# The last operand sums of a short-convolution kernel's head, chained through PSUM banks

## The chip, the cores and the metric

The kernel runs on one core of a Trainium2 chip. The metric is the device time of one execution in microseconds; less is better. Engines are named as in the profile: PE (TensorE), DVE (VectorE), ACT (ScalarE), POOL (GpSimd), SP (SyncE, which here only issues DMAs). Each engine works through its own queue in order; across engines an instruction waits on semaphores.

## What is computed

One layer, a gated short convolution between two RMS norms, in float32, for 1024 positions of width 1024:

```python
u = rms_norm(x, pre_norm)
z, bg, cg, v = jnp.split(u @ w_in, 4, axis=-1)       # w_in: 1024 x 8192
y = bg * causal_dwconv(cg * v, conv_w) * silu(z)     # 3 taps, 2048 channels
out = x + rms_norm(y @ w_out, post_norm)             # w_out: 2048 x 1024
```

## The kernel before

**Splitting.** A float32 product is made of three matmuls (`pass3`, lines 122 to 125): each operand is split into a high part (`high_u`, a cast on ACT) and a low part (`low_u`, a subtraction on DVE or POOL), and low x high, high x low and high x high add up in a PSUM bank.

**Head.** x is normalised, transposed on PE and kept as eight blocks bgh of [128, 2, 512] (g: a quarter of the 1024 inputs, h: a half of the positions); `read_k` makes a block's high part on ACT and its low part on DVE out of the transposes' PSUM banks pk, and `rebuild_a` copies the sum of both back from the bank into xa or xb (h = 0 or 1) on ACT; for h = 0 `rebuild` does it from the two parts on POOL. Meanwhile the first four column groups of w_in (the four kinds of the first 128 channels) are multiplied in full (`plain`, banks pp). All this is written out by hand as one program order, lines 591 to 719.

**Triples.** The other 60 column groups are taken in 20 triples. A triple's product, 2 halves by 4 quarters by 3 groups, is made of 20 products in place of 24, each of a sum of weight blocks (wA to wJ, two products each, split by `split_w`) and a sum of blocks of x, the form u_i. Seven of the 20 take a block as it is (`UNIT`, `B`); 13 need a form: 7, 9, 5 and 8, made in PSUM from the transposes' banks (`form`, `turned`), and 0, 17, 6, 4, 11, 16, 10, 2 and 19, kept as raw sums in SBUF. `stage(i)` names the place of such a sum: two to a tile by the table `PLACE`, in the pool `up`, which has 18 buffers and also holds the blocks, the forms' split parts u_i and the first weights; 19 stands in a buffer of the pool `raw`. `make` (lines 572 to 575) computes a sum, half by half. The forms of `LATE` (6, 4, 11, 16, 10, 2, 19) are split during the first triple, one after every second product (lines 811 to 815), so their raw sums live until then, and each later u_i takes the buffer of `up` that comes free. In PSUM there are eight banks, handed on in turn.

**The seam.** At line 720 the head's pool is closed; the weights' tiles wA and on take the room of xa and xb. So wA's cast on ACT (line 223) waits for the last sum that reads xa or xb. Then come the weights of the first triple (A to D), the gate and the three convolution taps of the first 128 channels (lines 728 to 735) and the first triple's products in the order `ORDER_0`: 7, 9, 1, 8, 3, 5, 14, 18, 0, 13, 17, 6, 4, 11, 15, 16, 10, 2, 12, 19, each adding into one of the banks pX, pY, pV, pZ, pW (`CHAINS`). `read` takes a bank's interim state off (lines 334 to 355), and the next product into that bank waits for the read. Two of these reads come up below: g <- pX ahead of product 18, and gc <- pY ahead of product 15.

Of the kernel before, what the change touches and what calls it, by code (L numbers as in the profile page):

```python
# [12 lines left out]
ALU = mybir.AluOpType  # L13
# [6 lines left out]
def kernel(  # L20
# [11 lines left out]
    nc = tc.nc  # L32
    P = 128
    _, L, D = x.shape
# [28 lines left out]
    def bank(name):  # L63
        return psum.tile([P, HB], F32, tag="bank", name=name)
# [44 lines left out]
    def new_u(name):  # L109
        return up.tile([P, 2, 2, HB], F32R, tag="u", name=name)  # L110
# [48 lines left out]
    def sums(t, steps):  # L159

        if t >= len(TRIPLES):
            return
        w0, w1, w2 = (ws[t, j] for j in range(3))
        if t not in es:
            es[t] = EP[t % 2].tile([P, 6, FC], F32, tag="e", name=f"e_{t}")
        e = es[t]
        add, sub = nc.gpsimd.tensor_add, nc.gpsimd.tensor_sub
        todo = {
            0: lambda: (add(w2[:, 0], w2[:, 0], w2[:, 1]), add(w2[:, 2], w2[:, 1], w2[:, 2])),  # L169
            1: lambda: sub(e[:, 0:2], w2[:, 0::2], w0[:, 0::2]),  # L170
            2: lambda: sub(e[:, 2], e[:, 1], w0[:, 3]),
            3: lambda: add(w1[:, 2], w2[:, 2], w1[:, 2]),
            4: lambda: sub(e[:, 3], w1[:, 2], w1[:, 0]),
            5: lambda: (sub(w0[:, 2], e[:, 3], w0[:, 2]), sub(w0[:, 0], e[:, 3], w0[:, 0])),  # L174
            6: lambda: sub(w0[:, 2], w0[:, 2], w0[:, 3]),
            7: lambda: sub(e[:, 4], w2[:, 1], w2[:, 3]),
            8: lambda: sub(e[:, 5], e[:, 4], w1[:, 3]),
            9: lambda: add(w2[:, 3], w1[:, 3], w2[:, 3]),
            10: lambda: sub(w1[:, 3], w1[:, 3], e[:, 2]),
            11: lambda: sub(w2[:, 3], e[:, 0], w2[:, 3]),  # L180
            12: lambda: sub(e[:, 3], e[:, 5], w1[:, 0]),  # L181
            13: lambda: add(w1[:, 0], w1[:, 0], w1[:, 1]),
            14: lambda: sub(e[:, 2], e[:, 0], w0[:, 3]),
            15: lambda: sub(w0[:, 3], w0[:, 3], w0[:, 1]),
        }
        for s in steps:
            todo[s]()
# [55 lines left out]
    def wide(pool, tag, name):  # L243
        return pool.tile([P, TAPS - 1 + HB], F32, tag=tag, name=name, bufs=5)

    def inner(t):
        return t[:, TAPS - 1 :]
# [31 lines left out]
    def cv_of(c, h):  # L279
        return inner(gts[c, h])  # L280
# [13 lines left out]
    def pad(c):  # L294
        nc.gpsimd.tensor_copy(gts[c, 1][:, : TAPS - 1], gts[c, 0][:, HB:])

    def gate_g(c, h, src, sign, direct):
        g = cv_of(c, h)
        if direct:
            nc.vector.scalar_tensor_tensor(g, src, float(sign), g, op0=ALU.mult, op1=ALU.mult)  # L300
        else:
            nc.gpsimd.tensor_mul(g, src, g)  # L302
        if h == 0:
            pad(c)
# [122 lines left out]
    gcol = small.tile([P, NK], F32, tag="gcol", name="gcol", bufs=1)  # L427
# [9 lines left out]
    gneg = snp.tile([P, 24], F32, tag="gneg", name="gneg", bufs=1)  # L437
# [35 lines left out]
    def read_k(k, h):  # L473

        g, kk = k // 2, k % 2
        if kk == 0:
            B[g, h] = new_u(f"b{g}{h}")
        u, src, gc = B[g, h], pk[k, h], gcol[:, k : k + 1]
        nc.scalar.activation(u[:, 0, kk], src, AF.Copy, scale=gc)
        nc.vector.scalar_tensor_tensor(u[:, 1, kk], src, gc, u[:, 0, kk].bitcast(F32), op0=ALU.mult, op1=ALU.subtract)  # L480

    def by_tile(a):
        return a.rearrange("p (t l) -> p t l", t=TH)
# [7 lines left out]
    def block(g, h):  # L491
        return (xa, xb)[h][:, :, 2 * g * P : 2 * (g + 1) * P].rearrange("p t (k l) -> p k t l", k=2)

    def as_block(u):
        return u.rearrange("p k (t l) -> p k t l", t=TH)

    plain_w, plain_ps, plain_k = {}, {}, {}
# [13 lines left out]
    def plain(n, h, ks):  # L511

        w = plain_w[n]
        for k in ks:
            first = (n, h) not in plain_ps
            if first:
                plain_ps[n, h] = bank(f"pp_{n}_{h}")
                plain_k[n, h] = 0
            plain_k[n, h] += 1
            hi, lo = (w[:, z, k * P : (k + 1) * P] for z in (0, 1))  # L520
            pass3(plain_ps[n, h], hi, lo, B[k // 2, h], k % 2, first, plain_k[n, h] == NK)

    def snap(n, h, gate=False):
        t = wide(snp, "sn", f"sp_{n}_{h}")
        if gate:
            gts[0, h] = t
        nc.scalar.activation(inner(t), plain_ps[n, h], AF.Silu if n == 2 else AF.Copy)
        return inner(t)
# [4 lines left out]
                turn(k, t)  # L533

    STAGE = {}
    PLACE = {0: (0, 0), 17: (0, 1), 6: (1, 0), 4: (1, 1), 11: (2, 0), 16: (2, 1), 10: (3, 0), 2: (3, 1)}

    def stage(i):
        if i == 19:
            if i not in STAGE:  # L540
                STAGE[i] = raw.tile([P, 2, HB], F32, tag="raw", name="s_19")
            return as_block(STAGE[i])
        n, j = PLACE[i]
        if n not in STAGE:
            STAGE[n] = up.tile([P, 2, 2, HB], F32, tag="u", name=f"s_{n}")
        return as_block(STAGE[n][:, j])

    FORM = {}

    def form(i, make, at=None):  # L550
        FORM[i] = at or [bank(f"f_{i}_{kk}") for kk in range(2)]
        for kk in range(2):
            make(by_tile(FORM[i][kk]), kk)

    def high_u(i):
        U[i] = u = new_u(f"u_{i}")
        for kk in range(2):
            if i in FORM:
                nc.scalar.copy(u[:, 0, kk], FORM[i][kk])
            else:  # L560
                nc.scalar.copy(as_block(u[:, 0])[:, kk], stage(i)[:, kk])

    def low_u(i, eng=nc.vector):
        u = U[i]
        for kk in range(2):
            if i in FORM:
                nc.vector.tensor_sub(u[:, 1, kk], FORM[i][kk], u[:, 0, kk].bitcast(F32))
            else:
                eng.tensor_sub(as_block(u[:, 1])[:, kk], stage(i)[:, kk], as_block(u[:, 0])[:, kk].bitcast(F32))
        FORM.pop(i, None)  # L570

    def make(eng, dst, kind, a, b):

        for kk in range(2):
            (eng.tensor_add if kind == "+" else eng.tensor_sub)(dst[:, kk], a[:, kk], b[:, kk])

    def turned(k, n, other, op):

        def do(dst, kk):
            nc.vector.scalar_tensor_tensor(dst, by_tile(pk[k + kk, 1]), n[:, k + kk : k + kk + 1], other[:, kk], op0=ALU.mult, op1=op)  # L580

        return do
# [4 lines left out]
    b00, b10, b20, b30 = (block(g, 0) for g in range(4))  # L587
    b01, b11, b21, b31 = (block(g, 1) for g in range(4))
# [83 lines left out]
    turn2((0, 1))  # L672
    for k in (0, 1):
        read_k(k, 1)
    low_u(5)
    plain(3, 0, range(KH, NK))
    turn2((6, 7))
# [1 line left out]
        rebuild_a(k, 1)  # L679
    for k in (6, 7):  # L680
        read_k(k, 1)
    form(8, lambda dst, kk: nc.vector.tensor_add(dst, b00[:, kk], b20[:, kk]))
    sn0[3] = snap(3, 0)
    plain(0, 1, (4, 5, 0, 1))
# [12 lines left out]
    for k in (2, 3):  # L697
        rebuild(nc.gpsimd, k, 0)
    make(nc.gpsimd, stage(0), "-", b30, b20)
    make(nc.gpsimd, b10, "+", b10, stage(0))  # L700
    form("q", turned(2, gcol, b21, ALU.subtract))
    q = [by_tile(a) for a in FORM.pop("q")]
    for n in (2, 3):
        plain(n, 1, (4, 5, 0, 1, 6, 7, 2, 3))
    for kk in range(2):
        nc.vector.tensor_add(stage(19)[:, kk], q[kk], b31[:, kk])
    for kk in range(2):
        nc.vector.tensor_sub(stage(16)[:, kk], q[kk], b01[:, kk])
    make(nc.vector, stage(6), "-", b01, stage(19))
    make(nc.vector, stage(17), "+", stage(6), b30)  # L710
    make(nc.vector, stage(11), "-", stage(6), b00)
    make(nc.gpsimd, stage(4), "-", b31, b30)
    make(nc.vector, stage(2), "+", stage(11), b10)
    make(nc.vector, stage(10), "-", b00, b01)
    nc.gpsimd.tensor_mul(inner(gts[0, 0]), inner(gts[0, 0]), sn0[1])
    snap(0, 1, True)
    pad(0)
    high_u(0)
    low_u(0, nc.gpsimd)
# [5 lines left out]
        split_w(0, unit)  # L725
        run_lows()
    sums(0, range(12, 16))
    gate_g(0, 1, plain_ps[1, 1], 1, True)
    high_u(17)
    low_u(17, nc.gpsimd)  # L730
    first_tap(0, 0)
# [256 lines left out]
```

## Time and profile before

| | us |
|---|---|
| median of 3 runs | 783.01 (782.99 to 783.21) |
| the profiled execution | 782.63 |
| its span in the trace | 780.8 |
| PE busy / DVE / ACT / POOL | 762.8 / 494.5 / 447.7 / 465.7 |
| mean granted clock of PE | 0.997 |

A row of a timeline has the start from the span's beginning, the length in us, engine, line, operation, output <- inputs and count; a row with x2 covers two instructions from the first start to the last end. In brackets stands the engine's idle time before it and what ended it. Names are without buffer numbers: s is a raw sum, f a form in PSUM, u a split form, b a block. A row of the groups has the busy time, the mean ns of one and the idle time before them.

### The profile page before, as it was taken

The numbers are of one execution on the slowest core, as the hardware profiler recorded it, in microseconds if no ns is written. First come the engines' busy times: TensorE is split into PE (matmuls) and PEld (weight loads), VectorE is DVE, ScalarE is ACT, GpSimd is POOL, SyncE is SP. The second block draws the span as 40 slices with busy tenths as digits, with TensorE's granted clock in tenths as the row PEclk, the third lists the DMA queues.
The fourth block names the chain that finished last, engine by engine and source line by source line (L and its number), as shares of the span: only waits on it lengthen the run. The fifth ranks groups of instructions, "written<-read, shape, count | busy, mean of one in ns | idle before, by whom it ended". The sixth has DMA issues, their size and how long they took to land.

```text
span 780.8 us, 10022 instructions
## 1 busy us (share of the span) xinstructions
PE 762.8 (98%) x3394; PEld 628.7 (81%) x3394; DVE 494.5 (63%) x750; ACT 447.7 (57%) x873; POOL 465.7 (60%) x565
## 2 busy tenths in 40 slices
PE   8998799999999999999999999999999999999996
PEld 8886588888888888888888888888888888888885
DVE  6898965656567566556565655565664957544756
ACT  7746665566565566645665755566565636544531
POOL 0698677687679669577877987896783320000020
PEclk9999999999999999999999999999999999999999
DMA  9400235536636445356368366665445779754237
GB/s 333 127 0 28 89 86 163 121 99 149 157 95 162 135 108 167 82 160 152 89 122 214 61 177 140 147 158 114 121 101 136 237 234 380 281 185 179 99 121 258
DMA packets 103219, 116.55 MB, mean 149 GB/s; under 512 B 4680, under 2 KB 70272, under 8 KB 102144
## 3 DMA queue, kind: packets, MB, share of 16 engines
q1 hardware_dynamic: 93936, 99.13, 38.6%
q0 software_dynamic: 9216, 16.78, 13.8%
q8 instruction: 26, 0.43, 0.2%
q14 instruction: 25, 0.20, 0.1%
q10 hardware_dynamic: 16, 0.00, 0.0%
HBM read 97.02 MB, written 44.04 MB: 181 GB/s over the span
## 4 chain that ended last, share of the span: by engine, by line
PE 89%; DVE 5%; ACT 4%; issue 1%; DMA 0%; DVEq 0%; ACTq 0%
PE pX L124 8%; PE pX L125 8%; PE pX L123 8%; PE pY L123 7%; PE pY L124 7%; PE pY L125 7%; PE po_x L865 4%; PE po_x L866 4%; PE po_x L867 4%; PE pV L123 3%; PE pV L124 3%; PE pV L125 3%; PE pZ L124 2%; PE pZ L123 2%; PE pZ L125 2%; PE pW L124 2%
## 5 line engine op out<-in xcount | busy, mean ns | idle before, releaser
L905 POOL TENSOR_TENSOR res<-xr,res 128x512 f32<-128x512 f32 x4 | 6.9, 1720 | 105.6 <-DVE res L904 105.6
L329 POOL TENSOR_TENSOR g<-g,sn 128x512 f32<-128x512 f32 x29 | 40.1, 1390 | 45.5 <-ACT sn L327 35.3
L353 DVE TENSOR_TENSOR sn<-sn,pY 128x512 f32<-128x512 f32 x57 | 39.2, 687 | 36.0 <-PE pY L125 21.7
L353 DVE TENSOR_TENSOR sn<-sn,pX 128x512 f32<-128x512 f32 x57 | 39.2, 688 | 34.9 <-PE pX L125 34.9
L302 POOL TENSOR_TENSOR g<-sn,g 128x512 f32<-128x512 f32 x23 | 29.9, 1301 | 47.5 <-DVE sn L351 47.5
L327 ACT ACTIVATE sn<-sn 128x512 f32<-128x512 f32 x24 | 15.2, 632 | 64.1 <-DVE sn L353 40.1
L311 POOL TENSOR_TENSOR g<-g,sn 128x512 f32<-128x512 f32 x20 | 28.2, 1412 | 18.0 <-DVE sn L353 17.7
L345 ACT COPY sn<-pZ 128x512 f32<-128x512 f32 x19 | 11.2, 589 | 46.6 <-PE pZ L125 44.0
L347 ACT ACTIVATE sn<-pV 128x512 f32<-128x512 f32 x38 | 20.7, 599 | 28.7 <-PE pV L125 28.7
L169 POOL TENSOR_TENSOR raw<-raw 128x256 f32<-128x256 f32 x40 | 32.6, 933 | 0.0
L359 POOL DMA_DIRECT2D s_d<-s_d x24 | 19.8, 825 | 21.0 <-DMA s_d<-y_d 13.4
L174 POOL TENSOR_TENSOR raw<-e,raw 128x256 f32<-128x256 f32 x40 | 29.2, 752 | 1.6
L351 DVE TENSOR_TENSOR g<-pY,g 128x512 f32<-128x512 f32 x15 | 10.4, 692 | 30.7 <-PE pY L125 30.7
L170 POOL TENSOR_TENSOR e<-raw,raw 128x512 f32<-128x512 f32 x20 | 25.9, 1294 | 1.6
L123 PE MATMUL pp<-b,wn 128*128 128x512 f32 x64 | 25.8, 403 | 0.1
L874 ACT ACTIVATE jk<-res 128x512 bf16<-128x512 f32 x12 | 7.6, 631 | 31.7 <-DVE res L932 13.0
L124 PE MATMUL pp<-b,wn 128*128 128x512 f32 x64 | 25.1, 393 | 0.4 <-DVE b L480 0.3
L125 PE MATMUL pp<-b,wn 128*128 128x512 f32 x64 | 25.0, 391 | 0.0
L181 POOL TENSOR_TENSOR e<-e,raw 128x256 f32<-128x256 f32 x20 | 14.8, 740 | 16.1 <-ACT wB L219 16.1
L292 DVE SCALAR_TENSOR_TENSOR g<-g,cw,cv 128x512 f32<-128x512 f32 x30 | 22.5, 749 | 1.8
L224 DVE TENSOR_TENSOR wD<-wD,wD 128x512 fp32r<-128x512 f32 x20 | 13.7, 684 | 15.0 <-ACT wD L223 15.0
L292 DVE SCALAR_TENSOR_TENSOR cv<-g,cw,cv 128x512 f32<-128x512 f32 x30 | 22.4, 748 | 0.0
(371 smaller groups left out, 2915.7 us busy)
## 6 DMA issues: line engine op xcount, KB each, us to landing
raw<-in_sc_w_in SPq DMA_DIRECT2D x64, 512.0 KB, 4.4
t_d<-in_sc_w_out SPq DMA_DIRECT2D x32, 256.0 KB, 4.6
s_d<-g SPq DMA_DIRECT2D x29, 256.0 KB, 2.1
s_d<-s_d POOLq DMA_DIRECT2D x24, 256.0 KB, 4.4
y_d<-g SPq DMA_DIRECT2D x23, 256.0 KB, 2.5
t_d<-in_sc_w_out POOLq DMA_DIRECT2D x16, 256.0 KB, 7.7
t_d<-t_d POOLq DMA_DIRECT2D x16, 256.0 KB, 4.5
xr<-in_x SPq DMA_DIRECT2D x8, 512.0 KB, 4.8
```

The lines of the kernel that those rows point to most:

```text
L123: nc.tensor.matmul(ps, lo, u[:, 0, kk], start=first, stop=False, skip_group_check=True)
L124: nc.tensor.matmul(ps, hi, u[:, 1, kk], start=False, stop=False, skip_group_check=True)
L125: nc.tensor.matmul(ps, hi, u[:, 0, kk], start=False, stop=last, skip_group_check=True)
L169: 0: lambda: (add(w2[:, 0], w2[:, 0], w2[:, 1]), add(w2[:, 2], w2[:, 1], w2[:, 2])),
L174: 5: lambda: (sub(w0[:, 2], e[:, 3], w0[:, 2]), sub(w0[:, 0], e[:, 3], w0[:, 0])),
L292: nc.vector.scalar_tensor_tensor(g if j == TAPS - 1 else ps, g, tap(c, j), ps, op0=ALU.mult, op1=ALU.add)
L302: nc.gpsimd.tensor_mul(g, src, g)
L329: when([(c, "cv", h), (c, "silu", h)], (c, "z", h), {"cv": 1, "silu": 1}, lambda: nc.gpsimd.tensor_mul(cv_of(c, h), cv_of(c, h), t))
L353: nc.vector.tensor_sub(a, a, ps)
L865: nc.tensor.matmul(ps, lo, u[:, 0, k % 2], start=first, stop=False, skip_group_check=True)
L866: nc.tensor.matmul(ps, hi, u[:, 1, k % 2], start=False, stop=False, skip_group_check=True)
L867: nc.tensor.matmul(ps, hi, u[:, 0, k % 2], start=False, stop=last, skip_group_check=True)
```

## The change

Forms 10 and 4 (b00 - b01 and b31 - b30) are made early, straight from the transposes' banks, behind `read_k` of the same block: two `scalar_tensor_tensor` each on DVE, the bank times the norm's weight (or its negative) plus or minus the other block. The sums 19, 6 and 11, each of which the next one uses, are made in PSUM banks (`banks_of`), the next sum reads the bank, and ACT copies the bank to the sum's place in SBUF (`keep`). The sum 4 is gone from POOL and the sum 10 from the end on DVE. The gate product of the first 128 channels' second half (`gate_g` at line 728) becomes a plain product on DVE between sums 17 and 11, and `snap(0, 1)` on ACT, which it needs, moves ahead of the sums. `PLACE` pairs the sums anew.

```diff
-    PLACE = {0: (0, 0), 17: (0, 1), 6: (1, 0), 4: (1, 1), 11: (2, 0), 16: (2, 1), 10: (3, 0), 2: (3, 1)}
+    PLACE = {10: (0, 0), 4: (0, 1), 0: (1, 0), 16: (1, 1), 6: (2, 0), 17: (2, 1), 11: (3, 0), 2: (3, 1)}
...
         for kk in range(2):
-            (eng.tensor_add if kind == "+" else eng.tensor_sub)(dst[:, kk], a[:, kk], b[:, kk])
+            d, x, y = (z[kk] if isinstance(z, list) else z[:, kk] for z in (dst, a, b))
+            (eng.tensor_add if kind == "+" else eng.tensor_sub)(d, x, y)
+
+    def keep(i):
+        for kk in range(2):
+            nc.scalar.copy(stage(i)[:, kk], by_tile(FORM[i][kk]))
+
+    def in_bank(i):
+        return [by_tile(a) for a in FORM[i]]
...
     for k in (0, 1):
         read_k(k, 1)
+    for kk in range(2):
+        turned(0, gneg, b00, ALU.add)(stage(10)[:, kk], kk)
     low_u(5)
...
     for k in (6, 7):
         read_k(k, 1)
+    for kk in range(2):
+        turned(6, gcol, b30, ALU.subtract)(stage(4)[:, kk], kk)
...
-    q = [by_tile(a) for a in FORM.pop("q")]
+    q = in_bank("q")
     for n in (2, 3):
         plain(n, 1, (4, 5, 0, 1, 6, 7, 2, 3))
-    for kk in range(2):
-        nc.vector.tensor_add(stage(19)[:, kk], q[kk], b31[:, kk])
-    for kk in range(2):
-        nc.vector.tensor_sub(stage(16)[:, kk], q[kk], b01[:, kk])
-    make(nc.vector, stage(6), "-", b01, stage(19))
-    make(nc.vector, stage(17), "+", stage(6), b30)
-    make(nc.vector, stage(11), "-", stage(6), b00)
-    make(nc.gpsimd, stage(4), "-", b31, b30)
-    make(nc.vector, stage(2), "+", stage(11), b10)
-    make(nc.vector, stage(10), "-", b00, b01)
+
+    def banks_of(i):
+        FORM[i] = [bank(f"f_{i}_{kk}") for kk in range(2)]
+        return in_bank(i)
+
+    snap(0, 1, True)
+    f19 = banks_of(19)
+    make(nc.vector, f19, "+", q, b31)
+    make(nc.vector, stage(16), "-", q, b01)
+    keep(19)
+    f6 = banks_of(6)
+    make(nc.vector, f6, "-", b01, f19)
+    keep(6)
+    make(nc.vector, stage(17), "+", f6, b30)
+    nc.vector.tensor_mul(cv_of(0, 1), plain_ps[1, 1], cv_of(0, 1))
+    f11 = banks_of(11)
+    make(nc.vector, f11, "-", f6, b00)
+    keep(11)
+    make(nc.vector, stage(2), "+", f11, b10)
+    FORM.clear()
     nc.gpsimd.tensor_mul(inner(gts[0, 0]), inner(gts[0, 0]), sn0[1])
-    snap(0, 1, True)
...
-    gate_g(0, 1, plain_ps[1, 1], 1, True)
```

**DVE, behind the reads of blocks b01 and b31 in the head.** Before (b_455 and b_486 are these blocks' low parts, u_429 is u_5, f_0_491 and f_1_492 are form 8):

```order
L480 SCALAR_TENSOR_TENSOR b_455<-pk_1_450,gcol,b_455 128x512
L567 TENSOR_TENSOR u_429<-pk_1_354,u_429 128x512
L567 TENSOR_TENSOR u_429<-pk_1_359,u_429 128x512
L480 SCALAR_TENSOR_TENSOR b_486<-pk_1_474,gcol,b_486 128x512
L480 SCALAR_TENSOR_TENSOR b_486<-pk_1_479,gcol,b_486 128x512
L682 TENSOR_TENSOR f_0_491<-xa 128x512
```

And now (s_460 is the tile of forms 10 and 4):

```order
L480 SCALAR_TENSOR_TENSOR b_455<-pk_1_450,gcol,b_455 128x512
L588 SCALAR_TENSOR_TENSOR s_460<-pk_1_445,gneg,xa 128x512
L588 SCALAR_TENSOR_TENSOR s_460<-pk_1_450,gneg,xa 128x512
L567 TENSOR_TENSOR u_429<-pk_1_354,u_429 128x512
L567 TENSOR_TENSOR u_429<-pk_1_359,u_429 128x512
L480 SCALAR_TENSOR_TENSOR b_489<-pk_1_477,gcol,b_489 128x512
L480 SCALAR_TENSOR_TENSOR b_489<-pk_1_482,gcol,b_489 128x512
L588 SCALAR_TENSOR_TENSOR s_460<-pk_1_477,gcol,xa 128x512
L588 SCALAR_TENSOR_TENSOR s_460<-pk_1_482,gcol,xa 128x512
L694 TENSOR_TENSOR f_0_496<-xa 128x512
```

Two operations stand ahead of u_5's low part, which frees two banks for PE, and two more ahead of form 8.

**DVE, the end of the head.** Before (s_651 is the tile of 6 and 4, s_586 that of 0 and 17, s_648 of 11 and 16, s_660 of 10 and 2):

```order
L575 TENSOR_TENSOR s_651<-xb,s_645 128x512 x2
L575 TENSOR_TENSOR s_586<-s_651,xa 128x512 x2
L575 TENSOR_TENSOR s_648<-s_651,xa 128x512 x2
L575 TENSOR_TENSOR s_660<-s_648,xa 128x512 x2
L575 TENSOR_TENSOR s_660<-xa,xb 128x512 x2
L224 TENSOR_TENSOR wA_684<-wA_685,wA_684 128x512
```

And now (f_0_661 and f_1_662 are sum 6 in its banks, f_0_671 and f_1_672 sum 11):

```order
L576 TENSOR_TENSOR f_0_661<-xb,f_0_652 128x512
L576 TENSOR_TENSOR f_1_662<-xb,f_1_653 128x512
L576 TENSOR_TENSOR s_665<-f_0_661,xa 128x512
L576 TENSOR_TENSOR s_665<-f_1_662,xa 128x512
L731 TENSOR_TENSOR sp_1_650<-pp_1_543,sp_1_650 128x512
L576 TENSOR_TENSOR f_0_671<-f_0_661,xa 128x512
L576 TENSOR_TENSOR f_1_672<-f_1_662,xa 128x512
L576 TENSOR_TENSOR s_675<-f_0_671,xa 128x512
L576 TENSOR_TENSOR s_675<-f_1_672,xa 128x512
L224 TENSOR_TENSOR wA_697<-wA_698,wA_697 128x512
```

Every sum has one input in a bank, the last pair is gone, and the gate product stands among them.

**ACT, between the last reads of the head and wA's cast.** Now (s_658, s_665 and s_675 are the places of 19, 6 and 11; u_682 is u_0); the six copies of L580 are new, and before the change u_0's casts and wA's copies stood right behind `snap(0, 1)`, the first row:

```order
L527 ACTIVATE sp_1_650<-pp_1_502 128x512
L580 COPY s_658<-f_0_652 128x512
L580 COPY s_658<-f_1_653 128x512
L580 COPY s_665<-f_0_661 128x512
L580 COPY s_665<-f_1_662 128x512
L580 COPY s_675<-f_0_671 128x512
L580 COPY s_675<-f_1_672 128x512
L561 CAST u_682<-s_591 128x512 x2
L221 COPY wA_698<-raw_3_140 128x256
L222 COPY wA_698<-raw_0_142 128x256
L223 CAST wA_697<-wA_698 128x512
```

So u_0's casts and wA's copies now come behind all the waits of the copies. Further on, in the first triple, ACT's order is the same, but two casts wait for other buffers: u_10's for DVE's subtraction of u_16, and u_2's, which waited for nothing, for DVE's subtraction of u_10, the last reader of the tile of 10 and 4.

## The prediction

> **What bounds the kernel now.** I read the page first, then the waits of TensorE (PE), then the timeline of each engine where those waits fall.
>
> ```profile
> PE 762.8 (98%) x3394; PEld 628.7 (81%) x3394; DVE 494.5 (63%) x750; ACT 447.7 (57%) x873; POOL 465.7 (60%) x565
> PE pX L123 <- DVE g L351: 3.4, 1, 3.4
> PE pV L123 <- DVE wB L224: 3.1, 1, 3.1
> PE pY L123 <- DVE wE L224: 0.7, 1, 0.7
> PE pY L123 <- DVE gc L353: 0.6, 1, 0.6
> 200.00:400.00 200.00, 199.78 (x881) 164.77 (x880) 119.85 (x182) 117.70 (x248) 148.06 (x187) 1.00 0.51 129
> ```
>
> PE is busy 98% of the span, and between 200 and 400 us (last row: busy PE first) 199.78 of 200. So a change to a helper engine can only win what PE waits, and its long waits are all for VectorE (DVE), all in the seam between the head and the first triple:
>
> ```profile
> 40.65 0.47 PE L123 MATMUL pp<-b,wn 128*128 128x512 f32 x1
> 47.59 0.50 PE L124 MATMUL pp<-b,wn 128*128 128x512 f32 x1
> 63.61 0.39 PE L125 MATMUL pp<-b,wn 128*128 128x512 f32 x1
> 67.09 0.47 PE L123 MATMUL pV<-u,wA 128*128 128x512 f32 x1 [3.10 <-DVE wB L224]
> 81.70 0.50 PE L123 MATMUL pX<-b,wD 128*128 128x512 f32 x1 [3.36 <-DVE g L351]
> 92.10 0.50 PE L123 MATMUL pY<-u,wF 128*128 128x512 f32 x1 [0.64 <-DVE gc L353]
> 94.97 0.39 PE L123 MATMUL pY<-b,wF 128*128 128x512 f32 x1
> ```
>
> Nearly 8 us are waited here. After 92.10 PE never waits again for long, so **the time moves by what the matmul at 92.10 and its next neighbours move**. Before it, DVE has no gap from 75.32 on; before that ScalarE (ACT) has none from 64.60 on, and ACT starts there because the head's last sum on DVE is over:
>
> ```profile
> 39.13 1.28 DVE L567 TENSOR_TENSOR u<-pk,u 128x512 fp32r<-128x512 f32 x2
> 41.22 1.41 DVE L480 SCALAR_TENSOR_TENSOR b<-pk,gcol,b 128x512 fp32r<-128x512 f32 x2 [0.81 <-ACT b L479]
> 42.55 1.83 DVE L682 TENSOR_TENSOR f<-xa 128x512 f32<-128x512 f32 x2
> 46.78 1.41 DVE L480 SCALAR_TENSOR_TENSOR b<-pk,gcol,b 128x512 fp32r<-128x512 f32 x2 [1.06 <-ACT b L479]
> 48.11 1.41 DVE L580 SCALAR_TENSOR_TENSOR f_q<-pk,gcol,xb 128x512 f32<-128x512 f32 x2
> 49.43 1.28 DVE L706 TENSOR_TENSOR s<-f_q,xb 128x512 f32<-128x512 f32 x2
> 50.62 1.28 DVE L708 TENSOR_TENSOR s<-f_q,xb 128x512 f32<-128x512 f32 x2
> 54.12 9.17 DVE L575 TENSOR_TENSOR s<-s,xa 128x512 f32<-128x512 f32 x6
> 63.21 1.28 DVE L575 TENSOR_TENSOR s<-xa,xb 128x512 f32<-128x512 f32 x2
> 53.21 1.14 ACT L561 CAST u<-s 128x512 fp32r<-128x512 f32 x2 [3.55 <-PE pp L125]
> 54.25 0.37 ACT L221 COPY wA<-raw 128x256 f32<-128x256 f32 x1
> 64.60 0.59 ACT L223 CAST wA<-wA 128x512 fp32r<-128x512 f32 x1 [9.57 <-DVE s L575]
> 48.11 2.55 POOL L575 TENSOR_TENSOR s<-xa 128x512 f32<-128x512 f32 x2
> ```
>
> The six sums at 54.12 have both inputs in SBUF and run beside GpSimd (POOL): 9.17 / 6 = 1.53 us each. The two at 63.21, alone, follow each other at about 0.60. L706 and L708 have one input in PSUM and run at (50.62 - 49.43) / 2 = 0.60 each, with POOL's 48.11 row beside them. That difference is what the change can win.
>
> **Step 1, what the two early forms cost.** The four new operations (10 and 4, made from the banks of the transposes) are like L580: (49.43 - 48.11) / 2 = 0.66 each. They stand in the head's tightest part, where DVE, ACT and PE pass banks to each other. The first pair stands before the row of 39.13: that goes to 40.45, its first half is done at 41.15, and PE's matmul of 40.65 needs the bank that it releases: PE +0.5. ACT's two copies out of the same banks now wait for the new pair, its casts behind them move by 0.6, and with them DVE's row of 41.22, to 41.8. Then comes the second pair, so L682 goes from 42.55 to 44.45 (+1.9). It has SBUF inputs and now meets POOL's 512-wide sums in place of 256-wide ones; it took 1.75 for two, its bounds are 1.2 (alone) and 3.06 (as at 54.12), and I take 2.1, near its own row. All behind it is then 2.3 late: ACT's casts of block 1, DVE's row of 46.78 (to 49.1), f_q (to 50.4), and PE, which waits for that row at 47.59 (to 49.9). PE's head ends at 66.15 in place of 63.85. Bounds of this step: 1.4 to 3.3.
>
> **Step 2, the chain.** From 50.4: f_q 2 x 0.66, sums 19 and 16 4 x 0.60, sum 6 2 x 0.60, so sum 6's first half is ready at 54.8. Sum 17 must wait until ACT has copied the half out of its bank (L345, a copy of PSUM to SBUF of the same size, below, has 0.57): it runs at 55.5 and 56.1, ending at 56.8. The gate product (0.60), sum 11 (2 x 0.60), ACT's copy and sum 2 follow; ACT's last copy ends at 59.25, DVE at 60.0, where it ended at 64.5. The two sums at 63.21 (form 10) are gone from DVE, form 4's from POOL. But ACT, a strict queue, now has the six copies ahead of u_0's casts and wA's copies, which it used to do while it waited: 54.25 - 53.21 = 1.04 and 0.8 more (two copies of 0.37, each with its issue), so wA's cast starts at 61.05 in place of 64.60: **3.55 earlier**. ACT, not DVE, sets that.
>
> The price of a sum with an operand or the result in PSUM is from these groups:
>
> ```profile
> L575 DVE TENSOR_TENSOR s<-s,xa 128x512 f32<-128x512 f32 x6 | 9.2, 1592 | 0.0
> L580 DVE SCALAR_TENSOR_TENSOR pk<-pk,gneg,xa 128x512 f32<-128x512 f32 x2 | 1.4, 751 | 0.0
> L575 DVE TENSOR_TENSOR s<-xa,xb 128x512 f32<-128x512 f32 x2 | 1.3, 679 | 0.0
> L708 DVE TENSOR_TENSOR s<-f_q,xb 128x512 f32<-128x512 f32 x2 | 1.3, 680 | 0.0
> ```
>
> PSUM in costs 680 ns against 679, and PSUM in and out 751 for the dearer kind, as its SBUF-bound kin. [...]
>
> **Step 3, the first triple.** ACT from 64.60 and DVE from 75.32 do the same work in the same order, only 3.55 earlier; DVE's gate of a half (0.60) has moved ahead, into the chain, where I counted it. POOL's late work is released by the same casts (wB, u_17) and moves along, so who runs beside whom stays. PE goes from the head straight on at 66.15 (its first product now waits for wA alone), is through product 14 at 75.75 and waits for g until 78.15: 2.4 in place of 3.36. Until then PE, late from step 1, has the least room: ACT's read of pV at 67.7 finds product 7 done with nothing to spare. From 78.15 PE follows DVE, 3.55 early.
>
> **Step 4, a new wait.** The forms have changed buffers: u_2's casts on ACT now take a buffer that DVE's u_10 subtraction must first give up.
>
> ```profile
> 88.87 1.97 DVE L569 TENSOR_TENSOR u<-s,u 128x512 fp32r<-128x512 f32 x2
> 91.97 0.68 DVE L224 TENSOR_TENSOR wI<-wI,wI 128x512 fp32r<-128x512 f32 x1
> 92.57 1.28 DVE L569 TENSOR_TENSOR u<-s,u 128x512 fp32r<-128x512 f32 x2
> 93.86 0.69 DVE L353 TENSOR_TENSOR gc<-gc,pY 128x512 f32<-128x512 f32 x1
> 89.52 1.12 ACT L561 CAST u<-s 128x512 fp32r<-128x512 f32 x2
> 91.59 0.57 ACT L345 COPY gc<-pZ 128x512 f32<-128x512 f32 x1
> ```
>
> In the old clock times: the casts go from 89.52 to 90.9 (end of 88.87's row), behind them wI's two copies end at 93.05 in place of 91.68, so DVE's row of 91.97 goes to 93.1, u_2's pair to 93.7 and the read of pY from 93.86 to 95.0, ending at 95.7. PE's matmul of 94.97 overwrites that bank: it starts at 95.75, with its slow first step **0.9 late**. Bounds: 0 (if something covers it) and 1.4 (the whole delay of the casts). Behind it, by the same reckoning, the next read that PE waits for comes out level with PE, and I find no second stall.
>
> **Sum.** -3.55 + 0.9 = -2.65. The profiled execution took 782.63 (span 780.8): it would be 780.0. The median shown, 783.01, is 0.4 above, so I give 780.4. With step 1 at its bounds the gain is 3.55 or 1.65; with step 4 at 0 it is 3.55.
>
> **Rivals.**
> - *The new wait costs nothing* (something hides it): 3.55 won, 779.5. Against: no slack in the rows above but 0.4 at 94.97. 0.13.
> - *PE becomes the bound.* If the granted clock drops behind the new gaps at 41 and 48 or later, PE arrives late in step 3, where ACT has no room:
>
> ```profile
> 67.40 0.39 PE L124 MATMUL pV<-u,wA 128*128 128x512 f32 x1
> 82.89 0.63 PE L124 MATMUL pX<-b,wD 128*128 128x512 f32 x1
> 80.00:90.00 10.00, 7.59 (x25) 5.75 (x26) 10.00 (x14) 4.34 (x10) 9.84 (x10) 0.83 0.21 79
> ```
>
>   After 3.1 us of waiting the matmuls kept 0.39, after 3.36 they took 0.63 and the slice's clock was 0.83; (1 - 0.83) x 10 = 1.7 us lost. The same loss ahead of product 7 leaves about 1 us of gain: 782.0. My longest gap is 2.4, so it needs a gap longer than I see. [...] 0.12.
> - *The port turns round* (the slower side). From 75.32 on DVE has twelve subtractions with two SBUF inputs, slowed more or less by what POOL does beside them:
>
> ```profile
> L569 DVE TENSOR_TENSOR u<-s,u 128x512 fp32r<-128x512 f32 x12 | 12.8, 1114 | 0.0
> ```
>
>   If POOL does not move along with DVE, they may come out at the 1592 ns of L575: 12 x 0.48 = 5.7 us more on a queue without a gap, so 786; from a mean of about 1335 ns on the gain is gone. (At the 679 of a sum alone they would give 5.2 more.) For it: nothing holds the two engines together but ACT. Against: POOL's work there is released by ACT's casts, as DVE's is. 0.08 beyond 784.6, and 0.07 for a smaller loss that ends within 0.2%.
> - *The chain was not what held ACT*, so nothing is won and the early forms' 2.3 us sit in PE's old slack of 3.1: 783. The wait of 9.57 at 64.60 speaks against it. 0.02.
>
> The forecast has the rest, 0.58. A measurement of this kernel tells about 0.2% (1.6 us) from no change: faster holds the forecast, the first rival and a little of the second (0.73), slower the port (0.08), the same the rest (0.19). The range, 779.0 to 782.5, takes the bounds of steps 1 and 4 and the second rival.
>
> **What would show it.** PE's first product at about 66, not 67.1, with no wait before it; a new wait of 2 us in all at 41 to 50; the chain's sums at 0.68 each, none at 1.5; ACT's wA cast at 61; the wait for g near 2.4, no slice with a lower clock; a new wait of 0.8 before pY<-b,wF near 91.5. I am wrong if L682 takes over 3 us, if the copies leave ACT later than 61.5, or if DVE's subtractions in the first triple change their durations.

## The result and the profile after

The changed kernel takes 780.56 us in the median of seven runs (780.39 to 780.83), against 782.99 (782.44 to 783.42) for the kernel before on the same chip: a ratio of 0.9969, 95% interval 0.9958 to 0.9981. On another chip it was 780.51 against 782.74 (0.9971, 0.9959 to 0.9982). The profiled execution took 780.58 (span 778.8), 2.05 less than that of before. PE's work is the same (first the page's busy times), and so is the middle of the program (then a window, busy PE first, the granted clock, DMA share and GB/s last):

```profile
PE 763.1 (98%) x3394; PEld 629.3 (81%) x3394; DVE 490.6 (63%) x752; ACT 451.2 (58%) x879; POOL 460.0 (59%) x563
```

```profile
200.00:400.00 200.00, 199.78 (x880) 164.81 (x879) 119.77 (x182) 117.78 (x247) 147.57 (x188) 1.00 0.51 130
```

PE's longest waits (us in all, times, the longest):

```profile
PE pX L123 <- DVE g L351: 2.3, 1, 2.3
PE pp L123 <- ACT b L479: 1.8, 2, 1.7
PE pY L123 <- DVE gc L353: 1.2, 2, 0.7
```

The 3.1 ahead of the first product is gone, the one for g is shorter, and there is a new one of 1.8 in the head. The timeline of PE has them in order:

```profile
49.68 0.49 PE L123 MATMUL pp<-b,wn 128*128 128x512 f32 x1 [1.66 <-ACT b L479]
50.47 0.50 PE L124 MATMUL pp<-b,wn 128*128 128x512 f32 x1 [0.29 <-DVE b L480]
...
66.68 0.39 PE L123 MATMUL pV<-u,wA 128*128 128x512 f32 x1
...
78.66 0.50 PE L123 MATMUL pX<-b,wD 128*128 128x512 f32 x1 [2.30 <-DVE g L351]
...
89.06 0.50 PE L123 MATMUL pY<-u,wF 128*128 128x512 f32 x1 [0.67 <-DVE gc L353]
...
92.60 0.50 PE L123 MATMUL pY<-b,wF 128*128 128x512 f32 x1 [0.52 <-DVE gc L353]
...
98.25 0.50 PE L123 MATMUL pX<-b,wJ 128*128 128x512 f32 x1
```

Held against the rows of before: the matmul that stood at 47.59 comes at 50.47, so PE is 2.9 late in the head (2.7 if counted from DVE's read of block b01, which starts at 37.97 in place of 37.81 though nothing ahead of it on DVE was changed); the first product starts without a wait at 66.68 (67.09); behind the wait for g PE is 81.70 - 78.66 = 3.04 early, at 89.06 still 3.04; at 92.60 only 2.37, and behind 98.25 some 2.0, which stays to the end. On DVE, ACT and POOL:

```profile
43.36 1.40 DVE L588 SCALAR_TENSOR_TENSOR s<-pk,gcol,xa 128x512 f32<-128x512 f32 x2
44.68 2.58 DVE L694 TENSOR_TENSOR f<-xa 128x512 f32<-128x512 f32 x2
44.96 3.43 POOL L501 TENSOR_TENSOR xa<-b 128x512 f32<-128x512 f32 x2
50.98 1.41 DVE L588 SCALAR_TENSOR_TENSOR f_q<-pk,gcol,xb 128x512 f32<-128x512 f32 x2
59.30 1.29 DVE L576 TENSOR_TENSOR s<-f,xa 128x512 f32<-128x512 f32 x2
61.55 0.59 ACT L223 CAST wA<-wA 128x512 fp32r<-128x512 f32 x1
72.35 5.06 DVE L569 TENSOR_TENSOR u<-s,u 128x512 fp32r<-128x512 f32 x4
87.84 1.14 ACT L561 CAST u<-s 128x512 fp32r<-128x512 f32 x2 [1.26 <-DVE u L569]
```

and the groups of the chain's sums and of the twelve subtractions (busy us, mean ns of one, idle before):

```profile
L576 DVE TENSOR_TENSOR s<-f,xa 128x512 f32<-128x512 f32 x4 | 2.6, 687 | 0.2
L576 DVE TENSOR_TENSOR f<-xb,f 128x512 f32<-128x512 f32 x2 | 1.3, 684 | 0.0
L569 DVE TENSOR_TENSOR u<-s,u 128x512 fp32r<-128x512 f32 x12 | 12.8, 1110 | 0.0
```

Form 8 (L694), which used to take 1.83 for its two sums, took 2.58, while POOL's rebuild of two half blocks beside it (L501) took 3.43. The chain ends on DVE at 60.6 (59.30 + 1.29), and wA's cast comes at 61.55 without a wait, so ACT's own queue sets it, 3.05 earlier than before. u_2's casts at 87.84 now wait 1.26.

### The profile page after: what moved, and what is told of

It reads as the page before. It is cut to its first block, busy times and chain, and to the rows that moved or that the text cites. A ratio compares the mean times of both kernels' runs of the same rounds, so it can differ in the third digit from the quotient of the medians.

```text
span 778.8 us, 10028 instructions
## 1 busy us (share of the span) xinstructions
PE 763.1 (98%) x3394; PEld 629.3 (81%) x3394; DVE 490.6 (63%) x752; ACT 451.2 (58%) x879; POOL 460.0 (59%) x563
## 4 chain that ended last, share of the span: by engine, by line
PE 88%; ACT 6%; DVE 5%; issue 1%; DMA 0%; DVEq 0%; ACTq 0%
PE pX L123 8%; PE pX L125 8%; PE pX L124 8%; PE pY L123 7%; PE pY L124 7%; PE pY L125 7%; PE po_x L887 4%; PE po_x L886 4%; PE po_x L885 4%; PE pV L123 3%; PE pV L125 3%; PE pV L124 3%; PE pZ L123 2%; PE pZ L124 2%; PE pZ L125 2%; PE pW L123 2%
```

## The experiments

The question after the result is which part of the change brings the 2 to 2.5 us, and what takes back the rest of the 3.04. My theory: the PSUM chain brings them, since it takes the head's last sums from 1.53 us to 0.6 each; the early forms cost the head 2.9, the new pairing 0.7 to 1. The first rival: the early forms bring it, by taking form 10 off DVE's end and form 4 off POOL.

All medians are of five runs, unless said, beside the kernel before on the same chip (782.70 to 782.74). In the table, "cast" is the start of wA's cast counted from DVE's read of block b01 (line 480), the last DVE row ahead of the change, which is at 37.7 to 38.3 in the different traces; "four" is the time of DVE's first four subtractions of the first triple (the row L569 x4 above), "g" is PE's wait for g.

| kernel | median | ratio (95%) | cast | four | g |
|---|---|---|---|---|---|
| before | 782.7 | | 26.8 | 5.12 | 3.36 |
| changed | 780.51 | 0.9971 (0.9959 to 0.9982) | 23.6 | 5.04 | 2.29 |
| chain alone | 779.60 | 0.9959 (0.9945 to 0.9972) | 23.4 | 5.10 | 3.36 |
| early forms alone | 780.16 | 0.9968 (0.9955 to 0.998) | 23.9 | 5.14 | 2.62 |
| changed, other pairing | 779.65 | 0.996 (0.9947 to 0.9972) | 23.9 | 3.39 | 0.64 |
| changed, u_0 first on ACT | 779.64 | 0.9962 (0.9949 to 0.9974) | 22.8 | 3.86 | 1.11 |
| changed, form 8 first | 779.18 | 0.9954 (0.9941 to 0.9966) | 21.8 | 5.03 | 2.27 |
| changed, all three | 776.80 | 0.9926 (0.9913 to 0.994) | 20.9 | 3.72 | 0.96 |
| before, u_0's low part later on POOL | 782.05 | 0.9991 (0.9982 to 1.0) | 24.6 | 6.06 | 4.28 |
| chain alone, form 10 on POOL | 778.47 | 0.9944 (0.9931 to 0.9956) | 20.4 | 6.09 | 3.34 |
| the same, POOL's gates later | 776.89 | 0.9924 (0.9911 to 0.9938) | 20.4 | 4.43 | 1.68 |
| all three, POOL's gates later | 776.80 | 0.9924 (0.9912 to 0.9937) | 20.9 | 2.49 | - |

### Each half by itself

The chain alone: the early forms are gone, form 4 is made on POOL and form 10 at DVE's end, as before the change, with the old pairing.

```diff
-    for kk in range(2):
-        turned(0, gneg, b00, ALU.add)(stage(10)[:, kk], kk)
...
-    for kk in range(2):
-        turned(6, gcol, b30, ALU.subtract)(stage(4)[:, kk], kk)
...
     make(nc.vector, f11, "-", f6, b00)
+    make(nc.gpsimd, stage(4), "-", b31, b30)
     keep(11)
     make(nc.vector, stage(2), "+", f11, b10)
+    make(nc.vector, stage(10), "-", b00, b01)
```

> The chain in PSUM banks without the two early forms: form 4 is back on POOL, form 10 at DVE's end, the old pairing of the sums. Theory (the gain is the PSUM chain, the early forms cost the head 2.9 us, the new pairing 0.7): the head is not delayed (PE's last head matmul at 63.8, f_q at 48.1), the chain's sums keep 0.64 to 0.68 us each even beside POOL, form 10 takes 1.2 to 1.6 for two, wA's cast starts at 59 to 60.5, u_2's casts do not wait for u_10; time 777.0 to 779.0, so 1.5 to 3.5 below the changed kernel. Rival (the early forms are what wins, since they take 2.5 us of sums off the end): wA's cast at 62 or later, time 781 or more. Rival (PE at 63.8 has no room to be earlier): wA early but the time no lower than 780.5.

Measured 779.60 (779.27 to 779.74). The head is not delayed and the chain's sums keep 0.64 to 0.69 us each beside POOL, as foreseen; but form 10 took 3.43 where 1.2 to 1.6 stood, the cast came at 61.56, and the time missed the expected 777.0 to 779.0. The chain's timeline on DVE, POOL and ACT ends so:

```profile
56.81 1.29 DVE L576 TENSOR_TENSOR s<-f,xa 128x512 f32<-128x512 f32 x2
58.02 3.43 DVE L576 TENSOR_TENSOR s<-xa,xb 128x512 f32<-128x512 f32 x2
57.91 2.99 POOL L569 TENSOR_TENSOR u<-s,u 128x512 fp32r<-128x512 f32 x2 [0.32 <-ACT u L561]
61.56 0.59 ACT L223 CAST wA<-wA 128x512 fp32r<-128x512 f32 x1 [2.52 <-DVE s L576]
```

The same pair of sums took 1.28 in the kernel before. The chain is over earlier now, so form 10 has moved beside POOL's u_0 (57.91), and both its inputs are in SBUF.

The early forms alone: the pairing and the four early operations of the change stay, the sums 19, 16, 6, 17, 11 and 2 are made in SBUF as before it (`snap(0, 1)` and the gate product go back to their old places, too).

```diff
-    f19 = banks_of(19)
-    make(nc.vector, f19, "+", q, b31)
...
-    keep(11)
-    make(nc.vector, stage(2), "+", f11, b10)
+    for kk in range(2):
+        nc.vector.tensor_add(stage(19)[:, kk], q[kk], b31[:, kk])
+    for kk in range(2):
+        nc.vector.tensor_sub(stage(16)[:, kk], q[kk], b01[:, kk])
+    make(nc.vector, stage(6), "-", b01, stage(19))
+    make(nc.vector, stage(17), "+", stage(6), b30)
+    make(nc.vector, stage(11), "-", stage(6), b00)
+    make(nc.vector, stage(2), "+", stage(11), b10)
```

> The two early forms alone: the five sums 19, 16, 6, 17, 11, 2 are made as before in SBUF, forms 10 and 4 are gone from the end, the pairing is the new one. Theory (the sums cost 1.53 us each because both inputs are in SBUF, beside whatever POOL does): DVE's end comes 2.9 later by the head and 1.3 earlier by form 10, wA's cast at 66, with the u_2 wait behind it: 785.0 (784 to 786). Rival (they cost 1.53 because of form 4's and the other sums on POOL, so that taking form 4 off POOL would have done most of it): POOL is idle from about 59 on, the last three or four sums take 0.65 each, wA's cast at 61.5 to 62.5, time 781.0 to 782.0.

Measured 780.16 (779.56 to 781.05): my theory's 785 fails, and the rival's mechanism is in the trace, with a time even below its 781. First the kernel before, where DVE's sums run beside POOL's:

```profile
52.42 1.78 DVE L575 TENSOR_TENSOR s<-xb,s 128x512 f32<-128x512 f32 x1
54.12 5.17 DVE L575 TENSOR_TENSOR s<-s,xa 128x512 f32<-128x512 f32 x3
53.61 3.43 POOL L575 TENSOR_TENSOR s<-xb,xa 128x512 f32<-128x512 f32 x2
59.30 3.44 POOL L569 TENSOR_TENSOR u<-s,u 128x512 fp32r<-128x512 f32 x2
```

and then the early forms alone:

```profile
54.56 1.28 DVE L576 TENSOR_TENSOR s<-xb,s 128x512 f32<-128x512 f32 x2
55.76 5.89 DVE L576 TENSOR_TENSOR s<-s,xa 128x512 f32<-128x512 f32 x6
56.96 3.48 DVE L576 TENSOR_TENSOR s<-s,xa 128x512 f32<-128x512 f32 x2
56.65 3.25 POOL L569 TENSOR_TENSOR u<-s,u 128x512 fp32r<-128x512 f32 x2 [1.36 <-ACT u L561]
```

In the first fence sums follow each other every 1.70 (52.42, 54.12), and POOL's operations of 512 take 3.43 / 2 = 1.72 each instead of 1.25 to 1.3 (in the changed kernel two sums on POOL took 2.50, a gate product 1.31). In the second, sum 6 at 54.56 has both inputs in SBUF and takes 0.6 per half, since POOL has little to do then; of the six behind it only the two that start at 56.96, beside POOL's u_0, have the 1.70 (3.48 for two, and 5.89 in all where before they were 9.17). So **the price of 1.53 was not the price of an operand in SBUF by itself. It was POOL beside it.** Form 4 off POOL, with sum 6 starting 2.7 later than before (54.56 against 51.82), takes away most of it, an operand in PSUM takes away the rest (0.64 to 0.69 a sum beside POOL in the chain alone), and both at once win nothing that one does not: 780.16 against 780.51. How the two engines hold each other up the rows do not show: the lone lengths of a sum and of an operation on POOL add up to 0.60 + 1.27 = 1.87 (an estimate, with 0.60 from the prediction's row at 63.21 and 1.27 from its row of 2.55 for two), and the measured 1.70 is 0.17 less.

### The price of POOL, from the other side

In the kernel before, only u_0's low part moves, to behind POOL's next four weight sums.

```diff
     high_u(0)
-    low_u(0, nc.gpsimd)
...
     sums(0, range(12, 16))
+    low_u(0, nc.gpsimd)
```

> The kernel before, with nothing in PSUM and no early forms: only POOL's two subtractions of u_0's low part stand later in POOL's order (behind its next four weight sums), so that they no longer run beside the head's last sums. Theory (a sum with both inputs in SBUF takes 0.60 us by itself and 1.70 beside a POOL operation of 512 elements; the place of its operands matters only then): DVE's sums from about 58.5 on take 0.60 to 0.68 each, form 10 ends at 61.5 to 62.5 in place of 64.5, wA's cast at about 62, time 780.5 (779.8 to 781.5), the head being as before. Rival (the operands' place is what costs; POOL's u_0 has no part in it): DVE's six sums keep 9.2 us in all, wA's cast at 64.6, time 782.5 to 783. Rival (the moved POOL work is late for the first triple or slows DVE there): DVE's sums faster, but time 782 or more.

Measured 782.05 (781.28 to 782.43, eleven runs). The group of six sums on DVE:

```profile
L575 DVE TENSOR_TENSOR s<-s,xa 128x512 f32<-128x512 f32 x6 | 7.0, 1227 | 0.0
```

The timeline of DVE, PE and POOL, with the four subtractions in the first triple, POOL's gate products beside them, product 18 behind the wait for g, and DVE's read of pX:

```profile
73.41 6.06 DVE L569 TENSOR_TENSOR u<-s,u 128x512 fp32r<-128x512 f32 x4
75.52 3.41 POOL L744 TENSOR_TENSOR sp<-sp,sp 128x512 f32<-128x512 f32 x2
80.73 0.80 PE L123 MATMUL pX<-b,wD 128*128 128x512 f32 x1 [4.28 <-DVE g L351]
83.69 0.69 DVE L353 TENSOR_TENSOR gc<-gc,pX 128x512 f32<-128x512 f32 x1 [0.66 <-PE pX L125]
```

With no operand in PSUM and no early form the six sums fall from 9.2 to 7.0 and the cast comes 2.2 earlier; the first rival is out. But the second rival holds for the time. The moved work itself is over (at 72.45) before the four subtractions begin (73.41), but it pushes POOL's later work back: the gate products (L744) now run wholly beside the four, which take 6.06 in place of 5.12. Product 18 is only 0.97 earlier (80.73 against 81.70). Behind the wait of 4.28 PE's clock then fell to 0.50 (80 to 85 us), DVE waited 0.66 for PE's pX, and at product 4 (pY<-u,wF) some 0.5 is left (91.57 against 92.10).

The chain alone, with form 10 on POOL behind form 4 and u_0's casts ahead of the copies of sum 11:

```diff
+    high_u(0)
     f11 = banks_of(11)
     make(nc.vector, f11, "-", f6, b00)
     make(nc.gpsimd, stage(4), "-", b31, b30)
+    make(nc.gpsimd, stage(10), "-", b00, b01)
     keep(11)
     make(nc.vector, stage(2), "+", f11, b10)
-    make(nc.vector, stage(10), "-", b00, b01)
...
-    high_u(0)
```

> The chain alone (as e1_chain_alone, no early forms), with form 10 on POOL behind form 4 in place of DVE's end, and u_0's casts on ACT ahead of the copies of sum 11. Theory (form 10 took 3.43 us at DVE's end because u_0's low part ran on POOL beside it; beside sums with an operand in a bank POOL runs at 2.56 for two and slows nothing): DVE's sums stay at 0.64 to 0.68 each, its last one ends at 58, POOL's form 10 at 58.6, wA's cast starts at 58.6 to 59 in place of 61.56, the head ends as before, PE goes straight on, and the time is 776.5 to 777.5. Rival (POOL's form 10 slows DVE's sums): cast at 60.5 or later, 778.5 or more. Rival (PE, which ends the head at 64.2, has no room left): cast at 58.7 but only 0.5 to 1.0 of it won, 778.5 to 779.2.

Measured 778.47 (777.63 to 778.81). In the seam everything is as the theory has it, POOL's form 10 at 2.56 beside DVE's sums at 0.64; yet only 1.1 of the 3 us that the cast gained over the chain alone reach the end. That is nearly the last rival's time but not its reason, since PE waits 3.34 for g and so has room:

```profile
58.48 0.59 ACT L223 CAST wA<-wA 128x512 fp32r<-128x512 f32 x1 [0.62 <-POOL s L576]
69.76 6.09 DVE L569 TENSOR_TENSOR u<-s,u 128x512 fp32r<-128x512 f32 x4
70.72 3.45 POOL L762 TENSOR_TENSOR sp<-sp,sp 128x512 f32<-128x512 f32 x2
77.11 0.80 PE L123 MATMUL pX<-b,wD 128*128 128x512 f32 x1 [3.34 <-DVE g L351]
```

The four subtractions take 6.09, a full 1.5 each, since POOL's two gate products (L762) and its weight sums run beside them from end to end. To test that, the two products go five products later in POOL's order (the loop's step 8 in place of 3):

```diff
-        if s == 3:
+        if s == 8:
             for h, t in ((0, sn0[2]), (1, silu1)):
```

> The kernel of e7_chain_form10_pool with POOL's two gate products of 512 (one row before the weight sums of the next triple, at 70.7 there) five products later in POOL's order. Theory (there the first triple came 3.1 us earlier, but DVE's four subtractions with both inputs in SBUF then ran wholly beside POOL, 6.09 us for four in place of 5.06 to 5.12, and most of the gain was given back at the wait for g): POOL now meets its wait for a transfer earlier and stands idle for one to two us beside them; the four take 3.7 to 4.8, g is read 1.3 to 2.4 earlier, PE's wait for g falls from 3.34 to 1 to 2, and as some of it comes back when the products run beside later subtractions, the time is 777.0 to 778.0. Rival (DVE's four are slow for another reason): still about 6.1 and 778.3 to 778.9.

Measured 776.89 (776.80 to 777.01), just below what was expected:

```profile
69.81 4.43 DVE L569 TENSOR_TENSOR u<-s,u 128x512 fp32r<-128x512 f32 x4
72.67 1.01 POOL L172 TENSOR_TENSOR raw<-raw,raw 128x256 f32<-128x256 f32 x1 [0.73 <-DMA raw<-in_sc_w_in]
75.49 0.50 PE L123 MATMUL pX<-b,wD 128*128 128x512 f32 x1 [1.68 <-DVE g L351]
```

POOL's operations there are shorter now (1.07 and 1.01 in place of 3.45 for the two products), and for 0.73 it waits for a transfer; the four fall to 4.43, the wait for g by 1.66, and the time by 1.6. The clock stayed at 1.00 this time, and a wait of DVE's for pX, 0.54 in the kernel before this one, is gone with it. This is the cause of most of what was given back, shown.

### The three costs of the change

Another pairing, in which u_2's casts wait for nothing new:

```diff
-    PLACE = {10: (0, 0), 4: (0, 1), 0: (1, 0), 16: (1, 1), 6: (2, 0), 17: (2, 1), 11: (3, 0), 2: (3, 1)}
+    PLACE = {10: (0, 0), 2: (0, 1), 4: (1, 0), 6: (1, 1), 0: (2, 0), 17: (2, 1), 11: (3, 0), 16: (3, 1)}
```

> The changed kernel with another pairing of the sums in the tiles (10 with 2, 4 with 6, 0 with 17, 11 with 16), so that u_2's casts no longer wait for DVE's subtraction of u_10. Theory (the new wait costs its 0.5 to 0.7 us at pY<-b,wF and about 0.3 behind it): up to there the trace is the same, that matmul waits at most 0.15, and the time is 779.7 (779.4 to 780.0), 0.6 to 1.1 below the changed kernel. Rival (the wait is paid back: the next matmuls wait for DVE anyway): less than 0.3 below, 780.3 to 780.7.

Measured 779.65 (779.35 to 779.89), 0.86 below the changed kernel, each held against its own chip's kernel before at nearly the same time. The wait is gone: DVE's two reads of pY stand 91.02 - 88.53 = 2.49 apart, where they stood 91.86 - 88.33 = 3.53 apart in the changed kernel:

```profile
88.33 0.67 DVE L353 TENSOR_TENSOR gc<-gc,pY 128x512 f32<-128x512 f32 x1
...
91.86 0.68 DVE L353 TENSOR_TENSOR gc<-gc,pY 128x512 f32<-128x512 f32 x1
```

But in the profiled execution the way there was not the same, which I had not expected. A window of the head, and the timeline of DVE, both with the other pairing:

```profile
50.00:55.00 5.00, 4.71 (x12) 3.50 (x13) 5.00 (x8) 2.10 (x4) 4.94 (x5) 0.66 0.00 0
```

```profile
74.30 3.39 DVE L569 TENSOR_TENSOR u<-s,u 128x512 fp32r<-128x512 f32 x4
88.53 0.67 DVE L353 TENSOR_TENSOR gc<-gc,pY 128x512 f32<-128x512 f32 x1
...
91.02 0.69 DVE L353 TENSOR_TENSOR gc<-gc,pY 128x512 f32<-128x512 f32 x1
```

PE's clock was 0.66 between 50 and 55 (the third number from the end), PE came late, DVE with it, and then the four subtractions missed POOL's busiest time (3.39 in place of 5.06), which made up for it in this execution.

u_0's casts first, in ACT's wait of 2.02 ahead of the copies of sum 11:

```diff
+    high_u(0)
     f11 = banks_of(11)
...
-    high_u(0)
     low_u(0, nc.gpsimd)
```

> The changed kernel with u_0's two casts moved on ACT ahead of the copies of sum 11 (they fall into the wait of 2.02 there). Theory (ACT, not DVE, sets wA's cast; DVE is done at 60.6, ACT would be at about 60.7): wA's cast starts at 60.5 to 60.8 in place of 61.55, the first triple comes 0.8 earlier, time 779.8 (779.5 to 780.1). Rival (DVE's last sum is what wA's cast waits for): cast at 61.4 or later, time as the changed kernel's, 780.4 to 780.8. Rival (PE, late from the head, has no room): cast at 60.7, but the wait for g shrinks and the time stays within 0.3 of the changed kernel.

Measured 779.64 (779.18 to 780.72; one of the five runs is as long as the changed kernel's). ACT's row:

```profile
60.69 0.59 ACT L223 CAST wA<-wA 128x512 fp32r<-128x512 f32 x1 [0.25 <-DVE s L576]
```

The cast comes 0.86 earlier and is released by DVE's last sum, as the theory has it: ACT's queue set it in the changed kernel.

Form 8 first, ahead of the second early pair:

```diff
+    form(8, lambda dst, kk: nc.vector.tensor_add(dst, b00[:, kk], b20[:, kk]))
     for kk in range(2):
         turned(6, gcol, b30, ALU.subtract)(stage(4)[:, kk], kk)
-    form(8, lambda dst, kk: nc.vector.tensor_add(dst, b00[:, kk], b20[:, kk]))
```

> The changed kernel with form 8 made ahead of the second early pair (form 4), where POOL still has its 256-wide sums, in place of behind it. Theory (form 8 took 2.58 us for two because POOL's 512-wide rebuild ran beside it, and that is why the head came 2.9 late and not the 2.3 foreseen): form 8 takes 1.3 to 1.85 for two, u_8's casts come earlier, PE's late start in the head is 1.9 to 2.3 in place of 2.9, the chain and wA's cast come 0.6 to 1.0 earlier, time 779.7 (779.4 to 780.1). Rival (the copies and reads of the banks behind the pair, not form 8, set the head's delay): the same 2.9 and 780.3 to 780.8.

Measured 779.18 (778.70 to 779.44), better than expected. PE's and DVE's rows:

```profile
48.55 0.50 PE L124 MATMUL pp<-b,wn 128*128 128x512 f32 x1 [0.28 <-DVE b L480]
43.24 1.85 DVE L692 TENSOR_TENSOR f<-xa 128x512 f32<-128x512 f32 x2
```

Form 8 is back at 1.85, and the wait of 1.66 for ACT is gone altogether: PE is 0.96 late in the head (48.55 against 47.59) in place of 2.9. Beside form 8's length it was, as far as one run that moved both can tell, its place: ACT's casts of u_8 wait for it (2.53 and 1.11 in the changed kernel, 1.03 and 0.56 here), and the next blocks' reads stand behind those casts.

All three together, and with POOL's gate products later as above:

> The changed kernel with all three mends: the pairing of e3_pairing, u_0's casts first as in e4_u0_first, form 8 first as in e8_form8_first. Theory (the terms add up as long as DVE and ACT, not PE, set the first triple): 0.6 for the pairing, 0.8 for ACT's order, 0.8 for form 8: 778.3 (777.8 to 778.9). Rival (with the head's end at 65.5 or later PE itself becomes the bound and the wait for g goes to nothing): 779.0 to 779.6, no better than one of them alone. Either way it stays above the chain with form 10 on POOL, which leaves the head as it was.

> The kernel of e9_three_mends with the same two gate products later on POOL. Theory: DVE's four subtractions, at 3.72 there, are near their floor of 2.5 and can win 0.3 to 1.0, the products then slow the next ones by 0.5 to 1.0: 776.3 to 777.0, no clear gain over e9_three_mends. Rival (POOL's wait for the transfer falls wholly on the four): 775.5 to 776.2.

Measured 776.80 (776.42 to 777.38) and 776.80 (776.70 to 777.35), the best times here with 776.89, some 3.7 below the changed kernel. The first beats its expectation of 778.3: the three gains by themselves add up to 0.86 + 0.87 + 1.33 = 3.06. Where the other 0.65 comes from is not shown: the four subtractions fall from 5.04 to 3.72, but they had fallen in two of the three kernels already. It also lies below the chain with form 10 on POOL (778.47), which its expectation had ruled out. In the second the four reach 2.49 and g makes nobody wait, but later subtractions pay (2.96 for a pair, and a wait of 1.65 for gc): the sum is the same, as expected.

The changed kernel once more:

> The changed kernel itself once more, for a comparison on the chip of these runs and a second profile. Every theory: 780.3 to 780.7, or 0.9969 of the kernel before. [...]

Measured 780.51 (780.27 to 780.83, six runs). The same five us in both profiles of the kernel, first the one above, then this one:

```profile
80.00:85.00 5.00, 4.66 (x14) 3.37 (x12) 5.00 (x7) 0.25 (x1) 5.00 (x5) 0.68 0.22 83
```

```profile
80.00:85.00 5.00, 3.07 (x13) 1.89 (x11) 5.00 (x8) 0.52 (x1) 5.00 (x5) 1.00 0.27 102
```

And PE's wait ahead of it, this time:

```profile
78.40 0.50 PE L123 MATMUL pX<-b,wD 128*128 128x512 f32 x1 [2.29 <-DVE g L351]
```

The same wait (2.30 and 2.29), once with the clock at 0.68 behind it and once at 1.00; executions of 780.58 and 780.35. At full clock PE waits that time away ahead of the next products (1.37 for u in place of 0.71).

## Why the prediction was right

The forecast of 780.4, faster, came true (780.56), and its mechanism, wA's cast earlier by the head's last sums, later losses at pY, is the one in the trace. How near the number came is partly luck. Between the profiled executions the forecast gain was 2.65 and the measured one 2.05 (782.63 to 780.58). The 780.4 fits because 0.4 was added for the kernel before, whose profiled execution lies below its median; the changed kernel's lies on its median.

- **Step 1** was mis-sized: "I take 2.1" for form 8, measured 2.58, and PE's delay is 2.9, not 2.3. That is inside its bounds (1.4 to 3.3), but these were bounds of form 8's length: with form 8 ahead of the pair 1.9 of the delay go, of which its length is 0.73 (2.58 against 1.85) and the rest, by subtraction, its place ahead of ACT's casts.
- **Step 2** was right as a length: from f_q to wA's cast 61.55 - 50.98 = 10.57, foreseen 61.05 - 50.4 = 10.65, and "ACT, not DVE, sets that" is shown. The sums have 0.64 to 0.69, no dearer by PSUM: 684 to 690 ns a piece against 679. But its reading, "that difference is what the change can win", was too narrow: the step names POOL beside the sums and then prices the operands' place, while POOL's form 4, which the change also takes away, was enough. The forecast stood; as an account of which part earns it, it fails.
- **Step 3** was right: everything 3.04 earlier (3.55 less step 1's error), the wait for g 2.30 (2.4), the twelve subtractions unchanged at 1110 ns (1114). "No slice with a lower clock" was wrong (0.68 between 80 and 85 us), at no cost.
- **Step 4** was right in sum, 3.04 - 2.03 = 1.01 against 0.9, and split in two: 0.79 at pY<-b,wF (a wait of 0.52 and slow first steps, 0.50 for a matmul in place of 0.39) and 0.22 at 98.25, where I found "no second stall".
- **Rivals.** *The new wait costs nothing* is refuted by the two reads of pY. *PE becomes the bound*: in the changed kernel the clock did drop, to 0.68 behind a wait of 2.30, but where PE had to wait anyway; in three kernels near it DVE did wait for the slowed PE's pX: 0.53 in the chain alone, 0.54 with form 10 on POOL, 0.66 with u_0's low part later. *The port turns round* did not happen in the change (1110 ns against 1114), and no run shows a port. What the runs show is DVE's four subtractions between 2.49 us (all three with the gates later, where POOL stands idle for 3.85 around them) and 6.09 (form 10 on POOL, which there ran beside them from end to end), and in two of these kernels that took much of a gain back. *The chain was not what held ACT* is refuted by every cast in the table.

## What to carry to other kernels

Before paying for another memory, look at what the neighbour does: where a group on one engine has a mean far above its lone duration (here 1592 ns against 679), ask first who runs beside it. Moving one operation of the other engine may win much of what the rewrite wins (here 2.2 us of head time for one moved line, against 3.2 for the change), though only 0.7 of it reached the end. When two remedies take away the same wait, try each alone. And a gain on a saturated stretch is only kept if the same pairs of engines do not meet again later: read the next contended group, not only the one that was mended.

## What was not expected of the hardware

The clock's drop follows only in part from the length of the wait. It came behind all four waits above 3.3: 3.36 before (0.76 between 80 and 85 us), 3.36 in the chain alone (0.81 between 75 and 80, 0.85 between 80 and 85), 3.34 with form 10 on POOL (the first matmul behind it took 0.80 us in place of 0.50) and 4.28 with u_0's low part later (0.50 between 80 and 85). Below that it came behind 2.30 (changed, first profile, 0.68) and 1.69 (the other pairing, in the head, 0.66), and did not come behind 3.10 (before, 1.00 between 65 and 70), 2.62 (early forms alone, 1.00 between 75 and 85), 2.29 (changed, second profile, 1.00), 2.27 (form 8 first, whose execution has a mean of 0.999) and another 1.69 (changed, second profile, in the head; a mean of 0.999, too). In the profile of the changed kernel the slow matmuls (0.63 us in place of 0.39) reach from 79.7 to 83.0, in that of the other pairing from 51.2 to 54.5, about 3.3 us both; behind the wait of 4.28 they last longer, from 80.7 to 86.0. What besides the wait's length decides whether the clock drops, these runs do not settle.
